# Neighbourhood attention in a hybrid layer: the value products of the tile behind move behind the scores of the next tile in TensorE's order

## The chip, the cores and the metric

The kernel runs on one core of a Trainium2 chip. The metric is the device time of one execution in microseconds (us). TensorE (PE, with its weight loads as PEld), VectorE (DVE), ScalarE (ACT), GpSimd (POOL) and SyncE (SP, which issues the DMAs) each work through a queue of their own.

## The reference, cut to what matters

The layer projects 1024 tokens and 16 meta tokens, runs latent attention (MLA) over 8 heads and neighbourhood attention (NA) over 16 heads of 64, gates both, projects and adds. The change is in the neighbourhood attention: each token of a 16 x 64 grid sees a window of 8 rows x 16 columns and the meta tokens.

```python
def row_block(args):
    r, q_row = args
    ...
    s_win = (jnp.einsum('bqhd,brqchd->bhqrc', q_row, k_win).astype(jnp.float32) * scale
             + bias.astype(jnp.float32)[None])
    s_meta = jnp.einsum('bqhd,bmhd->bhqm', q_row, k_meta).astype(jnp.float32) * scale + meta_b
    s = jnp.concatenate([s_win.reshape(B, NA_HEADS, GRID_W, n_win), s_meta], axis=-1)
    p = jax.nn.softmax(s, axis=-1).astype(v.dtype)
    ...
    return (jnp.einsum('bhqrc,brqchd->bqhd', p_win, v_win)
            + jnp.einsum('bhqm,bmhd->bqhd', p_meta, v_meta))
```

## The kernel before, in words

The program has a gate and setup stage (up to about 217 us), the neighbourhood stage (217 to 700 us), which the change touches, the latent attention and the output projection. Where operands are split, a rounded part (`h`, written by ScalarE, L481, L612, L158) and its rest (`l`, the difference, written by VectorE through the helper at L114) are multiplied apart, so that one product takes two or three matmuls.

The neighbourhood stage goes through 8 head pairs of 8 tiles of 128 queries: 64 tiles. Its loop (L718) takes one *step* per tile and overlaps several tiles in it. In step g:

- tile g+6 is projected to q, k and v (`part`, 24 matmuls into `ps_acc`, cut into the pieces 0 to 1, 1 to 4 and 4 to 8 of the 8 input chunks: 3, 9 and 12 matmuls). Its q and k are normalised (`na_acc`, `na_acc2`);
- tile g+3 has its q and k transposed (`na_tr`, `ps_tr<-raw`). ScalarE and VectorE split them: keys into `kM` (L481, rests at L114), queries into `qz` and `qs`;
- tile g+1 gets its scores (`na_qk`, `ps_s<-kM`, four matmuls, two for each head). They need the keys of the tile behind it, which `na_tr` transposed at the end of the step before. VectorE adds the bias and takes the minimum (L587), ScalarE takes the exponential (L592);
- tile g has its probabilities transposed, head by head (`na_ptr`, `ps_tr<-s_sb`); ScalarE casts them into `PT` (L612), VectorE writes their rest (L114). There are two `PT` buffers for each head, taken by turns (`PTS[j][t % 2]`);
- tile g-1 gets its value products (`na_pv`, L616, `ps_o<-PT`, six matmuls of 128 x 256). After every second tile ScalarE copies half of each bank (`u_na`, L638) and VectorE adds three times (L639, L640).

At the end of steps 3 and 7 of a pair the softmax sums of four tiles are spread and transposed too (`na_sum2`, `ps_tr<-rx`, copied by ScalarE as `nrp`, L662), and in step 1 the meta tokens are projected. The weights of the next pair are loaded and split (`w_split`, L151 to L160) over four steps. A step is numbered here by the tile that it projects, 0 to 7 in each pair.

What sets the order: TensorE's order is the order in which the program is written (`manual_schedule` for that engine alone). The queues of the other engines are ordered when the program is built, by a scheduler that starts from the order of the program and from times that it assumes, so a move on TensorE moves instructions on the others. Banks of PSUM: `ps_s` and `ps_tr` share four (tag `st`), `ps_o` has two and `ps_acc` two. A bank is taken again when its readers are done.

Of the kernel before, what the change touches and what calls it, by code (L numbers as in the profile page):

```python
# [21 lines left out]
NT = 8  # L22
# [27 lines left out]
def hybrid_layer(ctx, tc, x, x_t, meta, meta_t, norm_w, w_na, w_g, w_lat, lat_w, w_uq, w_ukv, vec128, qpe_w, kpe_w,  # L50
# [65 lines left out]
    def mm(o, l, r, start, stop):  # L116
        T.matmul(o, lhsT=l, rhs=r, start=start, stop=stop, skip_group_check=True)  # L117
# [323 lines left out]
    PTS = [[np1.tile([P, 3, 2, P], F32R, name=f"PT{j}{k}") for k in range(2)] for j in range(2)]  # L441
# [130 lines left out]
    def na_qk(p, t):  # L572
        d = st[p]
        w = WE if edge(t) else WI
        k0 = KS * max(t - 1, 0) + NM
        bias = d["b0"] if t == 0 else d["b7"] if t == NT - 1 else d["bi"]
        if t % 4 == 0:
            d["sum", t // 4] = small.tile([P, 4, 2], F32, name="nsum", bufs=2)
        qz, qs = d["q"][t]
        for j in range(2):  # L580
            s_ps = bank("s")[:, :w]
            mm(s_ps, qz[:, j], d["kM"][:, j, k0:k0 + w], True, False)
            mm(s_ps, qs[:, j], d["kM"][:, j, k0:k0 + w], False, True)
            sb = np2.tile([P, WI], F32, name="s_sb", bufs=3)[:, :w]

            mn = small.tile([P, 1], F32, name="nmn")
            V.tensor_tensor_reduce(out=sb, in0=s_ps, in1=bias[:, j, :], scale=1.0, scalar=BIG,  # L587
                                   op0=ALU.add, op1=ALU.min, accum_out=mn)
            d["p", t, j] = sb, mn
        for j in range(2):  # L590
            sb, mn = d["p", t, j]
            S.activation(sb, sb, AF.Exp, scale=-1.0, bias=mn, accum_out=d["sum", t // 4][:, t % 4, j:j + 1])  # L592

    def na_ptr(p, t, j):

        d = st[p]
        sb = d["p", t, j][0]
        ps = bank("tr")[:, :384].rearrange("p (c n) -> p c n", c=3)
        pt = d["PT", j] = PTS[j][t % 2]
        if not edge(t):  # L600

            for n, c in enumerate((0, 272, 144)):
                tr(ps[:, n, :], sb[:, c:c + P])
            parts = ((P, 0, 3),)
        else:

            for n, c in enumerate((144, 0) if t == 0 else (0, 144)):
                tr(ps[:, n, :], sb[:, c:c + P])
            tr(ps[:NM, 2, :], sb[:, 128:144])
            parts = ((P, 0, 2), (NM, 2, 3))  # L610
        for n, c0, c1 in parts:
            S.copy(pt[:n, c0:c1, 0, :], ps[:n, c0:c1])  # L612
        for n, c0, c1 in parts:
            lo_of(pt[:n, c0:c1, 1, :], ps[:n, c0:c1], pt[:n, c0:c1, 0, :])

    def na_pv(p, t):  # L616
        d = st[p]
        i = t % 2
        if i == 0:
            d["o"] = [bank("o").rearrange("p (t n) -> p t n", t=2) for _ in range(2)]  # L620
        if edge(t):
            vs = ((d["V"][1 if t == 0 else t - 1], P), (d["V"][t], P), (d["Vm"], P))
        else:
            vs = ((d["V"][t - 1], P), (d["Vp", t], P), (d["V"][t], P))
        for j in range(2):
            for n, (v, k) in enumerate(vs):
                sm = v.rearrange("p (j a) d -> p j (a d)", j=2)
                mm(d["o"][j][:, i, :], sm[:k, j, :], d["PT", j][:k, n].rearrange("p a n -> p (a n)"), n == 0, n == 2)
        if i == 1:

            if t % 4 == 1:
                d["y", t // 4] = np2.tile([P, 4, P], F32, name="y_na")
            y = d["y", t // 4][:, t % 4 - 1:t % 4 + 1]
            u = np2.tile([P, 2, 2, P], F32, name="u_na", bufs=1)
            for j in range(2):
                a, b = slice(64 * j, 64 * j + 64), slice(64 - 64 * j, 128 - 64 * j)
                o = d["o"][j].rearrange("p t (a n) -> p t a n", a=2)
                S.copy(u[a], o[b])  # L638
                V.tensor_tensor(u[a], u[a], o[a], op=ALU.add)  # L639
            V.tensor_tensor(y, u[:, :, 0, :], u[:, :, 1, :], op=ALU.add)  # L640
# [77 lines left out]
    for g in range(-LEAD, NSTEP + 4):  # L718
        a, b, pr = g, g - 1, g + LEAD
        on = lambda s: 0 <= s < NSTEP  # L720
        part = lambda c0, c1: None
        p, t = divmod(pr, NT)
# [15 lines left out]
            na_meta2(p)  # L738
        if on(b - 1) and (b - 1) % 4 == 3:
            na_sum((b - 1) // NT, (b - 1) % NT // 4)  # L740
        if on(b):
            na_pv(*divmod(b, NT))
        if on(pr - 2) and pr % 2:
            na_acc2(*divmod(pr - 2, NT))
        if on(a):
# [1 line left out]
        part(1, 4)  # L747
        if on(a + 1):
            na_qk(*divmod(a + 1, NT))
        if on(a):  # L750
            na_ptr(*divmod(a, NT), 1)
        part(4, 8)
# [2 lines left out]
        if on(pr):  # L755
# [8 lines left out]
            if 1 < t < 6:  # L764
                k = t - 2
# [146 lines left out]
    for i in range(LEAD, NT + 1):  # L912
        t = order[i]
# [96 lines left out]
    with ExitStack() as mx_:  # L1010
# [116 lines left out]
        for s in range(NS + 3):  # L1127
            cur = s < NS
            h, t = divmod(s, NT)
# [8 lines left out]
            if NS - 10 <= s < NS - 3:  # L1138

                i = s - (NS - 10)  # L1140
                k = KO[i]
# [63 lines left out]
    with ExitStack() as ox:  # L1205
# [21 lines left out]
        for i, k in enumerate(KO[7:]):  # L1227
            if i == 0:
                a, b = KH[:, :D], KL[:, :D]
            elif i == 1:  # L1230
                a, b = (mk.tile([P, L], F32R, name=f"wok{j}", tag=f"mkT{j}")[:, :D] for j in range(2))
            elif i == 2:
                v = mk.tile([P, NT + 1, 2, P], F32R, name="wov", tag="mV").rearrange("p k a n -> p (k a n)")
                a, b = v[:, :D], v[:, D:2 * D]
            else:
                a = o1.tile([P, D], F32R, name=f"woh{k}")
                b = o1.tile([P, D], F32R, name=f"wol{k}")
# [124 lines left out]
```

## Time and profile before

| | |
|---|---|
| median of 3 runs | 1369.73 us (1367.43 to 1370.75) |
| the profiled execution's own time | 1367.42 us |
| its span, first to last instruction | 1365.6 us |
| mean granted clock of TensorE | 0.989 |
| busy share of the span | PE 96%, DVE 70%, ACT 59%, POOL 29% |
| neighbourhood stage, 225 to 650 us | a head pair takes some 61 us; TensorE busy 402.4 of 425 us |

Times in the trace count from the start of the span. Matmuls are pipelined: one of 384 columns is shown with 340 ns, the next starts 176 ns after it, so what a piece takes is read from start to start. The idle time in brackets behind an instruction counts from the shown end of the one before. The granted clock is a share of 2.4 GHz; 0.5 is the lower level, 1.2 GHz.

### The profile page before, as it was taken

What the parts mean: (1) busy time and instruction counts of PE and PEld (TensorE: products, weight loads), DVE (VectorE), ACT (ScalarE), POOL (GpSimd) and SP (SyncE); (2) the same over time, 40 slices, a digit from 0 to 9 for tenths busy, and PEclk for the clock granted to TensorE, in tenths of its full rate; (3) what the DMA queues carried; (4) which work ended last, traced back from release to release, by engine and by line L of the source; (5) the groups of instructions that cost most, each with busy time, mean ns of one, the idle gap of its engine ahead of it and who ended that gap; (6) DMA issues with size and microseconds to landing.
All of it is one profiled execution on the core that took longest, in us unless ns stands there. A gap on an engine that the chain in (4) does not pass through costs nothing.

```text
span 1365.6 us, 24617 instructions
## 1 busy us (share of the span) xinstructions
PE 1312.9 (96%) x8116; PEld 1212.4 (89%) x8116; DVE 962.3 (70%) x3100; ACT 808.7 (59%) x2263; POOL 402.2 (29%) x851
## 2 busy tenths in 40 slices
PE   9999999999999999999899889999999999999999
PEld 7888889889898988989789889999999999988887
DVE  4933246888888888888778988988997988641110
ACT  6622136677776778677756667777777777630110
POOL 4322112122121222112345536625734752000000
PEclk9999999999999999999999899999999999999999
DMA  9352641131212212111111110100100022254231
GB/s 342 124 172 81 210 138 40 54 88 44 74 41 74 67 55 79 59 56 32 51 49 38 43 36 17 40 28 21 36 28 24 31 82 76 78 171 130 73 105 47
DMA packets 82254, 103.59 MB, mean 76 GB/s; under 512 B 10311, under 2 KB 60871, under 8 KB 82007
## 3 DMA queue, kind: packets, MB, share of 16 engines
q1 hardware_dynamic: 82127, 102.02, 23.8%
q8 instruction: 64, 1.05, 0.3%
q14 instruction: 63, 0.52, 0.1%
HBM read 70.80 MB, written 24.90 MB: 70 GB/s over the span
## 4 chain that ended last, share of the span: by engine, by line
PE 71%; DVE 17%; ACT 5%; issue 3%; DMA 2%; POOL 1%; SPq 0%; ACTq 0%; POOLq 0%; DVEq 0%
PE ps_acc L117 20%; PE mps_acc L117 10%; PE ps_s L117 9%; PE mps_s L117 8%; PE mps_st L117 7%; PE mps_o L117 5%; PE ps_o L117 5%; PE mps_tr L120 4%; PE ps_tr L120 3%; DVE u_na L639 2%; DVE m_sb L1034 2%; DMA wnf<-in_w_na_dram 1%; DVE PT L114 1%; DVE qs L557 1%; ACT qz L554 1%
## 5 line engine op out<-in xcount | busy, mean ns | idle before, releaser
L93 POOL TENSOR_TENSOR rs_y<-rs_v,mhalf 128x1 f32<-128x1 f32 (+5 forms) x170 | 148.5, 877 | 119.0 <-DVE rs_v L89 92.4
L117 PE MATMUL ps_acc<-wnh,hT 128*128 128x384 f32 (+1 forms) x432 | 161.7, 374 | 1.5 <-DVE natl L681 1.5
L117 PE MATMUL ps_acc<-wnl,hT 128*128 128x384 f32 (+1 forms) x432 | 146.0, 338 | 0.0
L117 PE MATMUL ps_acc<-wnh,hTl 128*128 128x384 f32 (+1 forms) x432 | 145.6, 337 | 0.0
L558 POOL CAST qs<-qz 64x128 fp32r<-64x128 f32 x128 | 42.1, 329 | 321.3 <-ACT qz L554 310.2
L117 PE MATMUL mps_s<-mkT,mq 128*128 128x346 f32 (+1 forms) x576 | 132.6, 339 | 1.4 <-DVE mPT L114 1.0
L592 ACT ACTIVATE s_sb<-s_sb,nmn 128x400 f32<-128x400 f32 (+1 forms) x128 | 76.9, 601 | 59.6 <-DVE nmn L587 51.5
L1060 ACT CAST mPT<-mps_tr 128x512 fp32r<-128x512 f32 x128 | 74.4, 583 | 53.7 <-PE mps_tr L120 52.7
L117 PE MATMUL mps_o<-mPT,mV 128*128 128x256 f32 x768 | 106.2, 287 | 0.0
L1034 DVE TENSOR_SCALAR_CACHE_REDUCE m_sb<-mps_s 128x346 f32<-128x346 f32 (+1 forms) x192 | 97.3, 512 | 9.7 <-PE mps_s L117 7.5
L114 DVE TENSOR_TENSOR mPT<-mps_tr,mPT 128x512 fp32r<-128x512 f32 x128 | 87.6, 685 | 13.6 <-ACT mPT L1060 12.5
L117 PEld LDWEIGHTS mps_s<-mkT,mq 128*128 128x128 f32 x576 | 93.7, 193 | 3.2 <-DVE mPT L114 1.7
L117 PEld LDWEIGHTS mps_o<-mPT,mV 128*128 128x128 f32 x768 | 94.8, 189 | 0.2
L1043 ACT ACTIVATE m_sb<-m_sb,mnm 128x1040 f32<-128x1040 f32 x64 | 74.6, 1166 | 20.9 <-DVE mnm L1042 14.8
L117 PEld LDWEIGHTS ps_acc<-wnh,hT 128*128 128x128 f32 x432 | 83.3, 193 | 2.6 <-DVE natl L681 1.7
L117 PEld LDWEIGHTS ps_acc<-wnl,hT 128*128 128x128 f32 x432 | 83.3, 193 | 0.0
L117 PEld LDWEIGHTS ps_acc<-wnh,hTl 128*128 128x128 f32 x432 | 82.5, 191 | 0.0
L612 ACT CAST PT<-ps_tr 128x384 fp32r<-128x384 f32 (+2 forms) x160 | 62.1, 411 | 31.1 <-PE ps_tr L120 30.1
L120 PE MATMUL mps_tr<-ident,m_sb 128*128 128x128 f32 x512 | 76.9, 273 | 2.6 <-DVE mq L114 1.0
L114 DVE TENSOR_TENSOR PT<-ps_tr,PT 128x384 fp32r<-128x384 f32 (+2 forms) x160 | 72.1, 466 | 7.0 <-ACT PT L612 6.1
L117 PE MATMUL ps_o<-PT,Vt 128*128 128x256 f32 x256 | 60.1, 298 | 15.9 <-DVE PT L114 15.9
L114 POOL TENSOR_TENSOR wnl<-wnf,wnh 128x384 fp32r<-128x384 f32 (+2 forms) x62 | 53.0, 874 | 61.2 <-ACT wnh L160 55.0
(477 smaller groups left out, 3931.1 us busy)
## 6 DMA issues: line engine op xcount, KB each, us to landing
wnf<-in_w_na_dram SPq DMA_DIRECT2D x32, 384.0 KB, 3.3
g_d<-g SPq DMA_DIRECT2D x32, 256.0 KB, 2.6
wnf<-in_w_out_dram SPq DMA_DIRECT2D x32, 256.0 KB, 2.7
wnf<-in_w_g_dram SPq DMA_DIRECT2D x19, 384.0 KB, 5.5
Vp<-Vt SPq DMA_DIRECT2D x48, 112.0 KB, 2.2
yfo<-y_d SPq DMA_DIRECT2D x24, 192.0 KB, 2.8
gt<-g_d SPq DMA_DIRECT2D x16, 256.0 KB, 3.1
y_d<-y_na SPq DMA_DIRECT2D x16, 256.0 KB, 2.0
```

Of the source, the lines that this page charges most:

```text
L93: G.tensor_tensor(y, v, mhalf[:np_, :n], op=ALU.pow)
L114: eng.tensor_tensor(dst, src, f(hi), op=ALU.subtract)
L117: T.matmul(o, lhsT=l, rhs=r, start=start, stop=stop, skip_group_check=True)
L120: T.transpose(out=o, in_=i, identity=ident[: i.shape[0], : i.shape[0]])
L554: lambda: [S.activation(qz[i, j], ps[i, :P], AF.Copy, scale=qkwn[i]) for j, i in enumerate((slice(0, 64), slice(64, P)))])
L558: G.tensor_copy(qs[h_, j], qz[l_, j])
L592: S.activation(sb, sb, AF.Exp, scale=-1.0, bias=mn, accum_out=d["sum", t // 4][:, t % 4, j:j + 1])
L612: S.copy(pt[:n, c0:c1, 0, :], ps[:n, c0:c1])
L639: V.tensor_tensor(u[a], u[a], o[a], op=ALU.add)
L1034: V.tensor_scalar(st["sb", h, t][:, ks], s_ps, -SCALE, BIG, op0=ALU.mult, op1=ALU.min, accum_out=st["mx", h, t][:, b:b + 1])
L1043: S.activation(sb, sb, AF.Exp, scale=-1.0, bias=nm, accum_out=st["ms", h, t // 2][:, t % 2:t % 2 + 1])
L1060: S.copy(dh, ps)
```

## The change

In a step the value products of the tile behind (`na_pv`) come after the scores of the next tile (`na_qk`) and not before the transposes of head 0. Since the step's own `na_ptr` for head 0 now comes before them in the program, the dictionary that holds `PT` is keyed by the buffer too.

```diff
@@ na_ptr
-        pt = d["PT", j] = PTS[j][t % 2]
+        pt = d["PT", j, t % 2] = PTS[j][t % 2]
@@ na_pv
-                mm(d["o"][j][:, i, :], sm[:k, j, :], d["PT", j][:k, n].rearrange("p a n -> p (a n)"), n == 0, n == 2)
+                mm(d["o"][j][:, i, :], sm[:k, j, :], d["PT", j, i][:k, n].rearrange("p a n -> p (a n)"), n == 0, n == 2)
@@ the loop over steps
-        if on(b):
-            na_pv(*divmod(b, NT))
         if on(pr - 2) and pr % 2:
             na_acc2(*divmod(pr - 2, NT))
         if on(a):
...
         part(1, 4)
         if on(a + 1):
             na_qk(*divmod(a + 1, NT))
+        if on(b):
+            na_pv(*divmod(b, NT))
         if on(a):
             na_ptr(*divmod(a, NT), 1)
```

TensorE's order in step 1 of a head pair, before. The first row is the transpose that ends step 0; numbers are buffers (they differ between the two programs), `PT00` and `PT10` are the `PT` buffers of the two heads:

```order
L120 MATMUL ps_tr_3924<-ident_62,raw_3540 128x128 x2
...
L117 MATMUL ps_acc_3948<-wnh_3328,hTl0_94 128x384
L117 MATMUL ps_o_3952<-PT00_1661,Vt_3197 128x256
...
L117 MATMUL ps_o_3953<-PT10_1663,Vt_3313 128x256
L120 MATMUL ps_tr_3965<-ident_62,s_sb_3895 128x128 x3
L117 MATMUL ps_acc_3948<-wnh_3328,hT0_92 128x384
...
L117 MATMUL ps_s_3981<-kM_3027,qz2_1653 128x400
...
L117 MATMUL ps_s_3987<-kM_3027,qs_3827 128x400
L120 MATMUL ps_tr_3995<-ident_62,s_sb_3901 128x128 x3
```

And the same step now:

```order
L120 MATMUL ps_tr_3924<-ident_62,raw_3540 128x128 x2
...
L117 MATMUL ps_acc_3948<-wnh_3328,hTl0_94 128x384
L120 MATMUL ps_tr_3957<-ident_62,s_sb_3882 128x128 x3
L117 MATMUL ps_acc_3948<-wnh_3328,hT0_92 128x384
...
L117 MATMUL ps_s_3973<-kM_3027,qz2_1653 128x400
...
L117 MATMUL ps_s_3979<-kM_3027,qs_3827 128x400
L117 MATMUL ps_o_3987<-PT00_1661,Vt_3197 128x256
...
L117 MATMUL ps_o_3988<-PT10_1663,Vt_3313 128x256
L120 MATMUL ps_tr_3995<-ident_62,s_sb_3888 128x128 x3
```

The six value products moved behind nine projections, three transposes and the four scores; all else stands as it did.

VectorE's queue from the key rests of step 7 (first row) to those of step 0 (last row), before. `wnl` and `wnlx` are the weights' rests, `ISA` is the addition of the bias with the minimum (L587), `u_na` and `y_na` belong to the value products:

```order
L114 TENSOR_TENSOR kM_3027<-ps_tr_3824,kM_3027 64x128 x2
...
L114 TENSOR_TENSOR wnl_4381<-wnf_4378,wnh_4380 128x384
...
L639 TENSOR_TENSOR u_na_3871<-u_na_3871,ps_o_3764 64x512
L587 ISA s_sb_3895,nmn_3896<-ps_s_3892,bi_3658 128x400
...
L639 TENSOR_TENSOR u_na_3871<-u_na_3871,ps_o_3765 64x512
...
L587 ISA s_sb_3901,nmn_3902<-ps_s_3898,bi_3658 128x400
...
L114 TENSOR_TENSOR PT00_1661<-ps_tr_3877,PT00_1661 128x3x128
L114 TENSOR_TENSOR wnlx_4483<-wnf_4480,wnhx_4482 128x384
L114 TENSOR_TENSOR PT10_1663<-ps_tr_3906,PT10_1663 128x3x128
L640 TENSOR_TENSOR y_na_3870<-u_na_3871 128x256
...
L114 TENSOR_TENSOR kM_3027<-ps_tr_3924,kM_3027 64x128 x2
```

And now:

```order
L114 TENSOR_TENSOR kM_3027<-ps_tr_3824,kM_3027 64x128 x2
...
L114 TENSOR_TENSOR wnl_4381<-wnf_4378,wnh_4380 128x384 x2
...
L587 ISA s_sb_3882,nmn_3883<-ps_s_3879,bi_3658 128x400
...
L114 TENSOR_TENSOR PT00_1661<-ps_tr_3864,PT00_1661 128x3x128
L587 ISA s_sb_3888,nmn_3889<-ps_s_3885,bi_3658 128x400
...
L114 TENSOR_TENSOR wnlx_4483<-wnf_4480,wnhx_4482 128x384 x2
...
L639 TENSOR_TENSOR u_na_3900<-u_na_3900,ps_o_3798 64x512
L639 TENSOR_TENSOR u_na_3900<-u_na_3900,ps_o_3799 64x512
L114 TENSOR_TENSOR PT10_1663<-ps_tr_3906,PT10_1663 128x3x128
...
L114 TENSOR_TENSOR kM_3027<-ps_tr_3924,kM_3027 64x128 x2
```

The scheduler put the rest of head 0's `PT` and the scores' reductions ahead of `u_na`, one weight rest more into the stretch, and `y_na` behind it (it follows the last row).

ScalarE's queue around the key casts of step 7 (`kM`, then `qz`), before:

```order
L460 CAST Vt_3840<-ps_acc_3754 128x2x64
L158 CAST wnh_4380<-wnf_4378 128x384
L481 CAST kM_3027<-ps_tr_3824 64x128 x2
L554 ACTIVATE qz2_1653<-ps_tr_3824,qkw_na_1649 64x128 x2
L158 CAST wnh_4380<-wnf_4378 128x384
L662 COPY nrp_3854<-ps_tr_3849 128x512
```

And now:

```order
L460 CAST Vt_3840<-ps_acc_3754 128x2x64
L481 CAST kM_3027<-ps_tr_3824 64x128 x2
L554 ACTIVATE qz2_1653<-ps_tr_3824,qkw_na_1649 64x128 x2
L158 CAST wnh_4380<-wnf_4378 128x384 x2
L662 COPY nrp_3854<-ps_tr_3849 128x512
```

The weight cast that stood ahead of the key casts stands behind them, next to its other half.

## Rows read from the trace of the kernel before

**Rows 1.** The page, busy time of each engine over the whole span, its share, and how many instructions.

```profile
PE 1312.9 (96%) x8116; PEld 1212.4 (89%) x8116; DVE 962.3 (70%) x3100; ACT 808.7 (59%) x2263; POOL 402.2 (29%) x851
```

**Rows 2.** Who waited for whom, TensorE's own waits between 195 and 700 us (microseconds in total, times, the longest).

```profile
PE ps_o L117 <- DVE PT L114: 15.9, 13, 2.1
PE ps_s L117 <- DVE kM L114: 5.4, 7, 2.4
PE ps_tr L120 <- DVE PT L114: 3.9, 7, 0.6
```

**Rows 3.** TensorE in order of time in one head pair (start in us, duration, engine, line, operation, tiles, shape, count; in brackets the idle time before and who ended it). `ps_acc` is a projection, `ps_o` the value products, `ps_s` the scores (with `hM`: the meta tokens' projection), `ps_tr` a transpose. The rows at 351.32, 359.10, 371.93, 399.20 and 405.73 are the first of steps 0, 1, 2, 6 and 7.

```profile
347.59 0.34 PE L117 MATMUL ps_s<-kM,qz 128*128 128x400 f32 x1
...
351.32 0.42 PE L117 MATMUL ps_acc<-wnh,hT 128*128 128x384 f32 x1
...
351.93 0.27 PE L117 MATMUL ps_o<-PT,Vt 128*128 128x256 f32 x1
...
352.74 0.49 PE L120 MATMUL ps_tr<-ident,s_sb 128*128 128x128 f32 x3
...
355.22 0.46 PE L117 MATMUL ps_s<-kM,qz 128*128 128x400 f32 x1 [0.42 <-DVE kM L114]
...
356.05 0.45 PE L117 MATMUL ps_s<-kM,qz 128*128 128x400 f32 x1 [0.19 <-ACT nrp L662]
...
359.10 0.42 PE L117 MATMUL ps_acc<-wnh,hT 128*128 128x384 f32 x1
...
361.96 0.39 PE L117 MATMUL ps_o<-PT,Vt 128*128 128x256 f32 x1 [2.09 <-DVE PT L114]
...
362.89 0.58 PE L117 MATMUL ps_o<-PT,Vt 128*128 128x256 f32 x1 [0.31 <-DVE PT L114]
...
369.98 0.36 PE L117 MATMUL ps_s<-wnh,hM 128*48 128x256 f32 x1
...
371.93 0.34 PE L117 MATMUL ps_acc<-wnh,hT 128*128 128x384 f32 x1
...
392.55 0.44 PE L120 MATMUL ps_tr<-ident,raw 128*128 128x128 f32 x2 [0.55 <-DVE PT L114]
...
399.20 0.42 PE L117 MATMUL ps_acc<-wnh,hT 128*128 128x384 f32 x1
...
402.43 0.34 PE L117 MATMUL ps_s<-kM,qz 128*128 128x400 f32 x1
...
405.73 0.42 PE L117 MATMUL ps_acc<-wnh,hT 128*128 128x384 f32 x1
```

**Rows 4.** TensorE by stretch (the stretch, its length, busy time and instructions, granted clock as a share of 2.4 GHz, share of the DMA engines, GB/s), behind waits in four head pairs.

```profile
243.00:247.00 4.00, 3.97 (x26) 1.00 0.46 131
301.00:305.00 4.00, 2.70 (x17) 1.00 0.74 221
362.00:366.00 4.00, 3.69 (x15) 0.57 0.69 187
546.00:550.00 4.00, 3.55 (x14) 0.61 0.57 165
```

**Rows 5.** One stretch by engine (the stretch, its length, then busy time and instructions of PE, PEld, DVE, ACT and POOL, granted clock, DMA share, GB/s).

```profile
354.88:363.28 8.40, 5.47 (x29) 4.54 (x30) 8.13 (x22) 7.21 (x19) 1.67 (x5) 0.96 0.42 120
```

**Rows 6.** VectorE in order of time in the same head pair: the rests of the keys' split, two instructions (one for each head) in a row; the one at 388.36 is of the meta tokens' keys.

```profile
346.75 0.61 DVE L114 TENSOR_TENSOR kM<-ps_tr,kM 64x128 fp32r<-64x128 f32 x2 [0.48 <-ACT qz L554]
...
354.88 0.61 DVE L114 TENSOR_TENSOR kM<-ps_tr,kM 64x128 fp32r<-64x128 f32 x2 [0.65 <-ACT qz L554]
...
388.36 0.59 DVE L114 TENSOR_TENSOR kM<-ps_tr,kM 64x128 fp32r<-64x128 f32 x2
...
401.30 0.61 DVE L114 TENSOR_TENSOR kM<-ps_tr,kM 64x128 fp32r<-64x128 f32 x2 [0.66 <-ACT qz L554]
```

**Rows 7.** ScalarE in order of time at the end of step 7 and in step 0 of the same head pair.

```profile
352.52 0.28 ACT L460 CAST Vt<-ps_acc 128x128 fp32r<-128x128 f32 x1
...
353.13 0.51 ACT L158 CAST wnh<-wnf 128x384 fp32r<-128x384 f32 x1 [0.33 <-DMA wnf<-in_w_na_dram]
...
353.55 0.53 ACT L481 CAST kM<-ps_tr 64x128 fp32r<-64x128 f32 x2
...
355.41 0.59 ACT L662 COPY nrp<-ps_tr 128x512 f32<-128x512 f32 x1
```

**Rows 8.** Groups of VectorE's instructions between 348 and 410 us (count, busy us, mean ns of one, idle us before them).

```profile
L114 DVE TENSOR_TENSOR wnl<-wnf,wnh 128x384 fp32r<-128x384 f32 x6 | 3.2, 552 | 0.3 <-ACT wnh L158 0.3
...
L640 DVE TENSOR_TENSOR y_na<-u_na 128x256 f32<-128x256 f32 x4 | 1.6, 412 | 0.0
```

**Rows 9.** TensorE in order of time, single waits in other head pairs.

```profile
243.03 0.39 PE L117 MATMUL ps_o<-PT,Vt 128*128 128x256 f32 x1 [1.46 <-DVE PT L114]
...
301.99 0.38 PE L117 MATMUL ps_o<-PT,Vt 128*128 128x256 f32 x1 [2.10 <-DVE PT L114]
...
601.44 0.45 PE L117 MATMUL ps_s<-kM,qz 128*128 128x400 f32 x1 [1.12 <-DVE kM L114]
...
660.73 0.45 PE L117 MATMUL ps_s<-kM,qz 128*128 128x400 f32 x1 [2.42 <-DVE kM L114]
...
666.13 0.42 PE L117 MATMUL ps_o<-PT,Vt 128*128 128x256 f32 x1 [1.53 <-DVE PT L114]
```

**Rows 10.** The same view as rows 8 for ScalarE between 225 and 700 us.

```profile
L638 ACT COPY u_na<-ps_o 64x512 f32<-64x512 f32 x64 | 37.2, 581 | 5.0 <-PE ps_o L117 3.6
```

## The prediction

> **What bounds the kernel now.** I read the engines' busy shares first, then TensorE's waits, then one head pair of the neighbourhood stage in order of time, then the clock and the other engines in the stretch where TensorE waits. TensorE is busy 96% of the span [rows 1], so a change pays only where TensorE stands still or runs slowly. Between 195 and 700 us it stands still before its value products for 15.9 us in 13 places, always for the rest part of the transposed probabilities (`PT`) from VectorE; before the scores 5.4 us for the rest part of the keys (`kM`); before the transposes 3.9 us for `PT` [rows 2]. [rows 3] are one head pair. I name a step by the tile it projects, 0 to 7. A step without a wait takes 405.73 - 399.20 = 6.53 us. Step 0 takes 359.10 - 351.32 = 7.78, so 1.25 too long (waits of 0.42 and 0.19, the rest restarts). Step 1 takes 371.93 - 359.10 = 12.83, of which 371.93 - 369.98 = 1.95 are meta products: 4.35 too long. In it stand the waits of 2.09 and 0.31, and a slow clock behind them: over 362 to 366 us the granted clock is 0.57 [rows 4], the half level of 1.2 GHz for most of it, which loses 4 x 0.43 = 1.7 us. The reader is to see that this step holds nearly all. Step 4 has the 0.55 at 392.55. Excess of the pair: 1.25 + 4.35 + 0.55 = 6.15 us.
>
> Why it waits: in steps 7 to 1 VectorE also splits the next head pair's weights. From the key rests at 354.88 to the next ones at 363.28 it is busy 8.13 of 8.40 us [rows 5], and the `PT` that the value products want stands late among that work.
>
> **The change part by part.** The value products (six matmuls, 352.74 - 351.93 = 0.81 us [rows 3]) move behind part 1 to 4 of the projection, the transposes of head 0 and the scores. TensorE's work is the same to the instruction.
>
> *What goes.* The value products now start later by what went ahead: from step start to scores 402.43 - 399.20 = 3.23 us, less 0.81 of their own and the first part's 0.6 that was ahead anyway, plus the scores' 0.73, is 2.5 us. Step 1's waits of 2.09 + 0.31 are below that, so by this alone they end. The 0.55 in step 4 waits for a PSUM bank that `PT` of head 0 still holds; 0.81 more lies between now, so it ends too.
>
> *What comes.* The scores come 0.81 us earlier and need the key rests from the step before. VectorE has the same work between two key rests, so the question is when that work starts and how it is queued.
> Step 7: scores were at 347.59 without a wait; at 346.78 they meet key rests that begin at 346.75 [rows 6] and take 0.61 for both heads, half of it for the first: wait 0.3, with restart 0.4.
> Step 0: before, ScalarE's key casts stood behind a weight cast that waited for its DMA (353.13), and began at 353.55 [rows 7]. In the changed order they come straight behind the `Vt` cast of 352.52, so at about 352.7, 0.85 earlier, and VectorE's key rests, which began 1.33 behind the casts, begin at 354.0 in place of 354.88. The scores (moved to 353.9) wait 0.3. The second head's scores wait for the bank that ScalarE frees with the copy `nrp`. It now stands behind both weight casts (0.42 each from start to start), which follow at 354.0, and takes 0.59: done at 355.4, where TensorE would be at 354.6. That wait grows from 0.19 to 0.8. With restarts 1.3, about as before.
> Step 1: VectorE's list from key rests to key rests loses a `y_na` (0.41) and gains a weight split (0.55 [rows 8]); a small `rs_y` that leaves and a small reciprocal that comes cancel. It is 8.5 us in place of 8.4, so the next key rests begin at 354.0 + 8.5 = 362.5 and the first head's are there at 362.8. TensorE reaches the scores at 351.6 (step 0's start, 0.3 late from step 7) + 6.53 + 1.3 + (3.23 - 0.81) = 361.8. Wait 1.0, with restart 1.1; then the value products follow at once, since their `PT` stands ahead of the key rests in the changed list. That is what is late next: the wait's owner changes and its size falls.
> Step 4: scores meet the meta keys' rests (388.36 [rows 6]), which read the bank that the second head wants: 0.8 in place of 0.55.
> Steps 2, 3, 5 and 6: the tightest is step 6, whose first head's key rests end at 401.30 + 0.3 = 401.6 [rows 6], 0.8 before its scores at 402.43: nothing.
> After: 0.4 + 1.3 + 1.1 + 0.8 = 3.6 us in place of 6.15.
>
> *The clock.* Behind waits of 2.1 it fell in four pairs (0.57 in the first, 0.61 in the last, over 4 us: some 1.6 us each), behind the 2.10 at 301.99 and the 1.46 at 243.03 it stayed at 1.00 [rows 4, 9]. A wait of 1.0 is nearest to the last: I price it at nothing; the other end is 1.6 us a pair.
>
> *The new wait's bounds.* The scores' wait for `kM` in step 1 is bounded below by the 0.42 of step 0 [rows 3], above by the 2.42 at 660.73 [rows 9], where ScalarE too was behind a DMA. The queue above gives 1.0; 0.4 would give 3 us more over five pairs, 2.4 with the slow clock takes the gain of step 1 away (rival 1).
>
> *What rides along.* Every second value step brings two ScalarE copies and three VectorE additions (`u_na`, `y_na`), which move with it; in the list above they are counted, behind the scores' reductions rather than ahead. It issues no DMA. The stores of `y` and loads of the gate follow `y_na` on SP's queue by some us, and nobody waits for them in this stage; `Vp` is wanted later than before. The `Vt` buffer that the value products free is next written after part 4 to 8, whose twelve matmuls lie between: hidden.
>
> *A rule against it.* These gaps repeat every head pair. The Trainium skill (Perfetto Trace Analysis, Optimization Strategy) says that the same gap repeating can mean that there is no SBUF or PSUM room for the next tile; by that a new order gives nothing and buffers are wanted. The trace agrees for the 0.55 (a bank), not for the 2.09, whose releaser is the data itself.
>
> **The sum.** Four pairs with the slow clock: 4 x (6.15 - 3.6) = 10.2. The pair at 302, without it: 0.9. The first pair has the 1.46 and a wait like the 0.55: I take half, 1.0. The pair at 601: its scores already wait 1.12 for `kM`, which grows by 0.8, and what goes before its value products and transposes is of that size: 0. The last tiles: the scores' 2.42 keeps its end, behind it the 1.53 at 666.13 goes, and a wait for key rests like step 1's comes, but the slow clock there may stay: 1.0 as an estimate between 0 and 1.9 (the 1.53 with a restart). Together 13.1. The profiled execution took 1367.4 us: 1354.3. It lay 2.3 us under the median of the runs (1369.7), so 1356.6, **1357 us**, for a median.
>
> **The rivals.**
> 1. *VectorE keeps the wait.* It works through 8.4 us without a gap whatever TensorE's order is; if its key rests of step 1 end as late as before (363.28 + 0.61 = 363.9 where TensorE wants them at 361.8), the scores wait 2.1 and the clock falls as it did. For it: the busy share of that stretch [rows 5]. Against it: the key casts are no longer behind the DMA. Then a pair gains 0 to 0.3, all in all 2 us: 1368. The Trainium skill (Perfetto Trace Analysis, Identifying the Most-Contended Engine) says to relieve the most-contended engine first; by that a new order on TensorE alone would give nothing. The trace agrees as far as the busy share of these steps goes.
> 2. *All waits end.* If ScalarE and VectorE run ahead since their inputs come 0.81 earlier, nothing replaces the 15.9 + 3.9 and the clock's 4 x 1.6: 26 us, 1344. Against it: the key rests.
> 3. *Slower: the `u_na` copies get ahead of the key casts.* In the changed order ScalarE's two copies out of PSUM (0.58 each [rows 10]) lie between scores and the step's key casts. If they wait for late value products and hold the key casts back by more than the 0.8 or so that the quiet steps have, each of the four steps a pair with copies loses about 0.81 + 1.16 - 0.8 = 1.2: 7 pairs x 4.7 = 33, less rival 2's 26: 7 us longer, 1377. For it: the copies' place. Against it: in the quiet steps ScalarE has gaps.
>
> **How the numbers follow.** Forecast 0.60, rival 1 0.20, rival 2 0.10, rival 3 0.10. A measurement of this kernel can tell about 0.3%, 4 us. The forecast and rival 2 are faster: 0.70; rival 1 the same: 0.20; rival 3 slower: 0.10. The forecast's own range is 1351 to 1363 (the new wait at 0.4 takes 3 off, all of the last tiles' waits 2 or so; the clock at its other end adds 6.5). To 8 in 10 the range takes in rival 1 and stops short of 2 and 3: 1347 to 1368.
>
> **What would show it.** Right: TensorE's waits before the value products near 0; before the scores for `kM` 12 to 16 us in 15 or more places, the longest of a regular pair near 1.0 us in step 1; granted clock 1.00 where it was 0.97; no wait of 0.55 before the transposes of step 4; `kM` casts on ScalarE ahead of the weight cast. Wrong: scores' waits of 2 us with a clock of 0.57 behind them (rival 1), or waits in steps 2, 3, 5 and 6 (rival 3).

## The result and the profile after

The changed kernel takes **1344.85 us** (median of 4 runs, 1344.31 to 1345.33) against 1368.88 of the kernel before beside it: ratio 0.983, interval 0.9817 to 0.9843. The profiled execution took 1344.79, 22.6 less than that of before. It is faster, as forecast, but by 24 us and not by 13, and it lies 2 us below the range. The time is that of rival 2, which had a chance of 0.10. The page and TensorE's own waits of after (microseconds, times, the longest), the counterparts of [rows 1, 2]:

```profile
span 1343.0 us, 24641 instructions
PE 1301.1 (97%) x8116; PEld 1202.7 (90%) x8116; DVE 956.9 (71%) x3100; ACT 806.5 (60%) x2263; POOL 398.2 (30%) x851
```

```profile
PE ps_s L117 <- DVE kM L114: 10.4, 10, 2.8
```

The 15.9 us before the value products are gone without a remainder, and so are the 3.9 before the transposes for `PT`. Before the scores 10.4 us for the keys stand in place of 5.4, in 10 places (the prediction's signs had 12 to 16 us in 15 or more). TensorE in order of time in the pair that answers to [rows 3]; the rows of `raw` are the transposes of queries and keys that end a step in both orders, here those that end steps 6, 7, 0 and 1 and the next step 6:

```profile
339.11 0.38 PE L120 MATMUL ps_tr<-ident,raw 128*128 128x128 f32 x2
...
341.75 0.36 PE L117 MATMUL ps_s<-kM,qz 128*128 128x400 f32 x1
...
345.68 0.38 PE L120 MATMUL ps_tr<-ident,raw 128*128 128x128 f32 x2
...
348.76 0.34 PE L117 MATMUL ps_s<-kM,qz 128*128 128x400 f32 x1
...
349.63 0.43 PE L117 MATMUL ps_s<-kM,qz 128*128 128x400 f32 x1 [0.35 <-DVE qs L557]
...
353.21 0.38 PE L120 MATMUL ps_tr<-ident,raw 128*128 128x128 f32 x2
...
356.89 0.45 PE L117 MATMUL ps_s<-kM,qz 128*128 128x400 f32 x1 [0.88 <-DVE kM L114]
...
360.88 0.38 PE L120 MATMUL ps_tr<-ident,raw 128*128 128x128 f32 x2
...
396.19 0.38 PE L120 MATMUL ps_tr<-ident,raw 128*128 128x128 f32 x2
```

Step 7 has no wait, step 0 one of 0.35 before the second head's scores, step 1 one of 0.88 for the keys, and nothing stands before the value products. The 0.35 ends with `qs`, VectorE's rests of the queries just transposed. These scores use queries that were transposed a step earlier, so by this reading they wait for a bank that `qs` reads, not for data. Behind the 0.88 the clock stays (stretch, length, then busy time and instructions of PE, PEld, DVE, ACT, POOL, granted clock, DMA share, GB/s), where [rows 4] had 0.57:

```profile
357.00:361.00 4.00, 4.00 (x27) 3.82 (x28) 3.92 (x13) 1.96 (x6) 0.00 (x0) 1.00 0.32 119
```

From one `raw` to the next I get the length of every step, in both kernels and all experiments (us, the pair at 340 to 410):

| kernel | step 7 | 0 | 1 | 2 | 3 | 4 | 5 | 6 | pair |
|---|---|---|---|---|---|---|---|---|---|
| before | 6.54 | 8.21 | 10.88 | 8.39 | 6.54 | 7.78 | 6.51 | 6.54 | 61.39 |
| changed | 6.57 | 7.53 | 7.67 | 8.39 | 6.52 | 7.33 | 6.50 | 6.57 | 57.08 |
| e1 value products late, scores as before | 6.54 | 7.68 | 7.82 | 8.39 | 6.53 | 7.08 | 6.86 | 6.52 | 57.42 |
| e2 move in step 1 alone | 6.55 | 8.16 | 8.64 | 8.38 | 6.53 | 7.78 | 6.47 | 6.53 | 59.04 |
| e3 move in all but step 1 | 6.57 | 7.55 | 8.70 | 8.40 | 6.52 | 7.31 | 6.51 | 6.57 | 58.13 |
| e4 changed, one chunk later | 6.79 | 7.58 | 7.73 | 8.37 | 6.52 | 7.79 | 6.28 | 6.54 | 57.60 |
| e4b changed, one chunk earlier | 6.70 | 7.15 | 8.45 | 8.42 | 6.88 | 7.72 | 7.37 | 7.09 | 59.78 |
| e5 changed, splits on GpSimd | 6.59 | 8.97 | 10.39 | 8.41 | 6.52 | 7.32 | 6.53 | 6.57 | 61.30 |
| e6 before, splits on GpSimd | 6.54 | 10.02 | 10.85 | 8.41 | 6.55 | 7.79 | 6.51 | 6.56 | 63.23 |
| e7 e1, both one chunk later | 6.50 | 6.99 | 7.96 | 8.59 | 6.50 | 7.00 | 6.59 | 6.51 | 56.64 |
| e8 changed, value products further back | 6.78 | 6.96 | 8.44 | 8.41 | 6.83 | 7.45 | 7.41 | 6.90 | 59.18 |
| e9 e1, scores alone a chunk later | 7.13 | 7.48 | 8.01 | 8.51 | 7.16 | 7.02 | 6.94 | 6.54 | 58.79 |

Over the stage, the same rows at the start of the first pair with the slow clock, behind the four such pairs, and the last of these rows, some steps before the stage ends, of before and (the first row is shown above, at 339.11) of after:

```profile
344.21 0.38 PE L120 MATMUL ps_tr<-ident,raw 128*128 128x128 f32 x2
...
589.83 0.38 PE L120 MATMUL ps_tr<-ident,raw 128*128 128x128 f32 x2
...
678.80 0.38 PE L120 MATMUL ps_tr<-ident,raw 128*128 128x128 f32 x2
```

```profile
567.79 0.38 PE L120 MATMUL ps_tr<-ident,raw 128*128 128x128 f32 x2
...
654.45 0.38 PE L120 MATMUL ps_tr<-ident,raw 128*128 128x128 f32 x2
```

Up to the first row 5.1 us are won (344.21 - 339.11), in the four pairs 16.9 (245.62 against 228.68), from there to the last row 2.3, together 24.35. Behind it 1.75 are lost again: the span ends 686.8 after the last row before, 688.55 now.

### The profile page after: what moved, and what is told of

Its sections match the earlier page's. It is cut to its first block, busy times and chain, and to the rows that moved or that the text cites. A ratio compares the mean times of both kernels' runs of the same rounds, so it can differ in the third digit from the quotient of the medians.

```text
span 1343.0 us, 24641 instructions
## 1 busy us (share of the span) xinstructions
PE 1301.1 (97%) x8116; PEld 1202.7 (90%) x8116; DVE 956.9 (71%) x3100; ACT 806.5 (60%) x2263; POOL 398.2 (30%) x851
## 4 chain that ended last, share of the span: by engine, by line
PE 61%; DVE 20%; ACT 11%; issue 4%; DMA 2%; POOL 1%; SPq 0%; ACTq 0%; DVEq 0%; POOLq 0%
PE ps_acc L117 14%; PE mps_acc L117 10%; PE mps_s L117 8%; PE ps_s L117 8%; PE mps_st L117 7%; PE mps_o L117 5%; PE mps_tr L120 4%; PE ps_o L117 3%; ACT s_sb L592 2%; DVE qs L557 2%; ACT qz L554 2%; PE ps_tr L120 2%; DVE s_sb L587 2%; DVE PT L114 2%; DVE m_sb L1034 2%
## 5 line engine op out<-in xcount | busy, mean ns | idle before, releaser
L558 POOL CAST qs<-qz 64x128 fp32r<-64x128 f32 x128 | 38.3, 299 | 339.5 <-ACT qz L554 327.1
L120 PEld LDWEIGHTS mps_tr<-ident,m_sb 128*128 128x128 f32 x512 | 60.9, 140 | 5.6 <-ACT wnh L160 1.3
```

Source lines behind the costliest of these rows:

```text
L120: T.transpose(out=o, in_=i, identity=ident[: i.shape[0], : i.shape[0]])
L558: G.tensor_copy(qs[h_, j], qz[l_, j])
```

## The experiments

**Theory A**, formed on the two traces: the scores do not meet key rests that stay where they were. The key casts stand on ScalarE behind the exponentials, these behind VectorE's reductions of the scores, so scores that come earlier bring the next step's keys earlier too; the loop moves as a whole. **Theory B**: only the value products' slack counts. **The prediction's rule**: rests stay, so a wait grows by what the scores gain.

**e1.** The value products move, the scores stay (they are behind part 1 to 4, ahead of the scores):

```diff
         part(1, 4)
+        if on(b):
+            na_pv(*divmod(b, NT))
         if on(a + 1):
             na_qk(*divmod(a + 1, NT))
-        if on(b):
-            na_pv(*divmod(b, NT))
```

> Theory A (the loop moves as a whole): scores that come earlier bring the exponentials, the key casts queued behind them on ScalarE, and with these the key rests of the next step earlier too; so moving the scores ahead of the value products costs no wait for keys. Theory B: the value products' slack alone did it, and the scores' place did nothing. Here the value products move behind part 1 to 4 but stay ahead of the scores, so they get 1.7 us of slack and the scores stay where they were. A: step 0 as before (8.1 us, with the waits of 0.3 to 0.45 and 0.2), step 1 about 8.0 (a rest of 0.4 to 0.7 of the wait for PT, then some 0.6 for the keys), step 4 7.3 to 7.8, clock 1.00; head pair 58.1 to 58.7 us, total 1352 to 1356. B: step 0 and 4 as in the changed kernel (7.55 and 7.33), head pair 57.3 to 57.8, total 1345 to 1349.

Measured 1340.59, ratio 0.9812 (0.9794 to 0.983); pair 57.42. The pair is B's, the total is below what either had. TensorE in order of time:

```profile
358.24 0.39 PE L117 MATMUL ps_o<-PT,Vt 128*128 128x256 f32 x1 [0.57 <-DVE PT L114]
```

Of the wait of 2.09 there is 0.57 left, as A said, but step 0 is 0.5 shorter than before though the scores stand where they stood: its wait for `kM` is gone, since ScalarE's weight cast no longer waits for its DMA there. So 4.0 of the 4.3 us that a pair gains come with the value products' move alone, and the scores' earlier place brings the other 0.3. By the ratios this kernel is 0.2% faster than the changed one, which the intervals do not tell apart. In the two traces it is ahead only behind the last row of `raw`, which lies at 655.62, 1.2 later (on what follows there, see e10b).

**e2 and e3.** The move in step 1 alone, and in all but step 1 (against the changed kernel):

```diff
+        if on(b) and pr % NT != 1:      # e3: == 1, at the old place
+            na_pv(*divmod(b, NT))
...
-        if on(b):
+        if on(b) and pr % NT == 1:      # e3: != 1, behind the scores
             na_pv(*divmod(b, NT))
```

> The value products follow the scores in step 1 of each head pair alone; in the other seven steps they stay ahead. If the steps' gains are separate terms, as the prediction summed them, step 1 takes 7.67 us as in the changed kernel, steps 0 and 4 stay at 8.13 and 7.78, head pair 58.1, total about 1352. Theory A: step 0's key rests stay late, VectorE's list of 8.4 us behind them starts late, and the scores of step 1 wait about 1.5 us in place of 0.88; step 1 about 8.3, head pair 58.7, total about 1356, or 1.6 more a pair if the clock falls behind a wait of 1.5 (1366).

> The reverse: the value products stay ahead of the scores in step 1 alone. Separate terms: step 1 keeps its 10.95 us with waits of 2.1 and 0.3 and a clock near 0.57 behind them; steps 0 and 4 at 7.55 and 7.33; head pair 60.3, total about 1362. Theory A: in steps 7 and 0 the scores and what hangs on them come earlier, VectorE's list behind the key rests of step 0 starts about 1 us earlier, so the wait for PT in step 1 falls from 2.1 to about 1.1 and the clock stays at 1.00: step 1 about 8.5 to 9.2, head pair 58 to 58.7, total 1350 to 1355.

Measured 1355.29 (0.9916, 0.9898 to 0.9933) and 1350.59 (0.9882, 0.9864 to 0.9899). Both times are A's. TensorE in step 1 of e2, then of e3 with its clock:

```profile
358.92 0.52 PE L120 MATMUL ps_tr<-ident,s_sb 128*128 128x128 f32 x3 [1.04 <-DVE nmn L587]
...
361.62 0.45 PE L117 MATMUL ps_s<-kM,qz 128*128 128x400 f32 x1 [0.59 <-DVE kM L114]
```

```profile
357.12 0.39 PE L117 MATMUL ps_o<-PT,Vt 128*128 128x256 f32 x1 [0.97 <-DVE u_na L639]
...
358.44 0.39 PE L117 MATMUL ps_o<-PT,Vt 128*128 128x256 f32 x1 [0.69 <-DVE PT L114]
```

```profile
358.00:362.00 4.00, 3.56 (x23) 3.53 (x24) 3.86 (x13) 1.10 (x2) 0.00 (x0) 1.00 0.65 237
```

In e2 step 1 loses 1.04 before the transposes (to the reduction of the scores) and 0.59 before the scores, not one wait of 1.5, since step 0 hands its delay on. In e3 the value products of step 1 stand at the old place, and yet the 2.09 has become 0.97 for the sums' additions (`u_na`) and 0.69 for `PT`, and the clock stays; in one of five pairs with these waits it fell (0.72 over 534 to 540 us). A pair gains 2.35 in e2 and 3.26 in e3, 5.6 together, where the whole move gains 4.3: the steps are no separate terms. The prediction carried step 0's keys into step 1, but took step 0's own keys from no step before it.

**e4 and e4b.** The changed kernel with scores and value products one chunk later, and one earlier:

```diff
-        part(1, 4)
+        part(1, 5)      # e4b: part(1, 3)
...
-        part(4, 8)
+        part(5, 8)      # e4b: part(3, 8)
```

> The changed kernel with scores and value products one chunk of the projection (three matmuls, 0.5 us) later. If the key rests stay where they are (the prediction's rule), step 1's wait of 0.88 for the keys falls to about 0.4 and step 0's 0.35 ends: 0.8 us a head pair, total about 1339 to 1341. Theory A: the key rests come 0.5 later with the scores, the wait in step 1 stays at 0.8 to 0.9 and that of step 0 at 0.3; total 1344 to 1347; the gap between key rests and scores in the quiet steps, 0.1 us in the changed kernel, grows to about 0.6.

> The changed kernel with scores and value products one chunk of the projection (0.5 us) earlier. Theory A with a floor: the keys of a step begin with its last transposes, and in the quiet steps the key rests already stand 2.24 us behind these with the scores 0.1 behind the first head's rest; 0.5 earlier the scores wait about 0.4 in each of the 60 steps, total 1362 to 1370. Theory A without a floor (all moves along): 1343 to 1347. The prediction's rule (rests fixed where they were): waits of 0.4 in the quiet steps and 1.3 in step 1, 1366 to 1373.

Measured 1345.67 (0.9843, 0.9826 to 0.986) and 1359.43 (0.9937, 0.9916 to 0.9958). In e4, step 0's key casts (ScalarE) and rests (VectorE), and the scores of steps 0 and 1:

```profile
348.63 0.54 ACT L481 CAST kM<-ps_tr 64x128 fp32r<-64x128 f32 x2
```

```profile
349.97 0.61 DVE L114 TENSOR_TENSOR kM<-ps_tr,kM 64x128 fp32r<-64x128 f32 x2 [0.52 <-ACT qz L554]
```

```profile
351.46 0.42 PE L117 MATMUL ps_s<-kM,qz 128*128 128x400 f32 x1 [0.40 <-DVE qs L557]
...
358.75 0.45 PE L117 MATMUL ps_s<-kM,qz 128*128 128x400 f32 x1 [0.89 <-DVE kM L114]
```

Against the transposes at 346.93 the casts come at 1.70 and the rests at 3.04; in the changed kernel (345.68) at 1.12 and 2.47. With scores 0.52 later the keys come 0.58 later, and the waits are 0.40 and 0.89 in place of 0.35 and 0.88. That is A, to a tenth, and against the prediction's rule. It holds in steps 7 to 1; in the quiet step behind the transposes at 391.20 the rests hardly move (2.32 us behind these, 2.24 in the changed kernel). e4b shows the floor:

```profile
394.13 0.40 PE L117 MATMUL ps_s<-kM,qz 128*128 128x272 f32 x1 [0.62 <-DVE kM L114]
...
401.13 0.45 PE L117 MATMUL ps_s<-kM,qz 128*128 128x400 f32 x1 [0.28 <-DVE kM L114]
```

With scores 0.5 earlier the key rests of these two quiet steps begin 2.60 and 2.24 us behind the transposes (391.19 and 398.56), no earlier than in the changed kernel (2.27 and 2.24), and the scores wait 0.62 and 0.28. It costs less than I had set (15 us and not 18 to 25), since not every step waits.

**e5, e6, e10.** Half of the next pair's weight splits on GpSimd in place of VectorE, in the changed kernel, in the kernel before and in e1:

```diff
-        d["w"].append(w_split(w_na[p, :, 2 * k:2 * k + 2, :], 384, (V, V), parts=True, own=wx if k == 3 else None))
+        d["w"].append(w_split(w_na[p, :, 2 * k:2 * k + 2, :], 384, (V, G), parts=True, own=wx if k == 3 else None))
```

> The changed kernel with the second half of each weight split of the next head pair on GpSimd in place of VectorE (four of eight splits a pair, 0.55 us each on VectorE). If what is left, 0.88 us before the scores of step 1 and 0.35 in step 0, is VectorE's backlog of splits: one to two splits less lie between the key rests of steps 0 and 1, the 0.88 falls to 0 to 0.3, step 1 about 6.9, head pair 56.2 to 56.5, total about 1338 to 1341. If it is TensorE's or ScalarE's chain that sets the keys: unchanged, 1344 to 1347. Rival: GpSimd's longer splits hold its copies of the queries back and the scores wait for them: slower, 1348 or more.

> The same on the kernel before, the value products ahead of the scores. If VectorE's backlog makes the wait of 2.1 before the value products of step 1: it falls by two to three splits to 0.5 to 1.0, the clock stays 1.00 in that step, step 1 about 8.3 to 8.8 in place of 10.95, head pair 58.5 to 59.5, total 1352 to 1358. If the wait is set by the place of the value products alone: 2.0 or more and a clock near 0.57 as before, total 1366 to 1370.

> The version with the value products behind part 1 to 4 and ahead of the scores, with the same splits on GpSimd. If the backlog makes its 0.57 before the value products of step 1: it ends, step 1 about 7.0 to 7.3, head pair 56.5 to 57, total about 1334 to 1338, the fastest so far. Else 1340.

Measured 1359.1 (0.994, 0.9924 to 0.9956), 1369.62 (1.0017, 1.0006 to 1.0028) and 1352.74 (0.9892, 0.9875 to 0.9908; no trace of it is read). None brings what a shorter list on VectorE was to bring: they lie 18, 12 and 15 us above that. The time of e5 is in its rival's range (1348 or more), but its scores wait for keys and not for queries. That of e6 is in the range for "the place of the value products alone", though the longest wait before these is 1.5 and not 2.0. e10 lies 13 us above even its other branch. Step 0 of e5 on ScalarE, its scores of steps 0 and 1 on TensorE, and the clock behind them:

```profile
353.88 0.52 ACT L158 CAST wnh<-wnf 128x384 fp32r<-128x384 f32 x1 [0.39 <-DMA wnf<-in_w_na_dram]
```

```profile
355.97 0.45 PE L117 MATMUL ps_s<-kM,qz 128*128 128x400 f32 x1 [1.30 <-DVE kM L114]
...
365.24 0.45 PE L117 MATMUL ps_s<-kM,qz 128*128 128x400 f32 x1 [2.04 <-DVE kM L114]
```

```profile
365.00:369.00 4.00, 3.76 (x16) 3.67 (x17) 3.00 (x11) 1.31 (x4) 0.00 (x0) 0.61 0.18 67
```

This is, in the changed order of TensorE, what the prediction feared: a weight cast that waits 0.39 for its DMA ahead of the key casts, which follow at 354.30, keys late in step 0 (1.30), late again in step 1 (2.04), and the slow clock. GpSimd takes 1.1 us in the mean for a split that VectorE does in 0.55; that the weight's buffer is thus free later for the next load would explain the waiting cast, but is not shown. VectorE gained nothing either (e5, VectorE, then GpSimd):

```profile
358.03 0.97 DVE L100 TENSOR_TENSOR rs_t<-rs_y 128x8 f32<-128x8 f32 x1
```

```profile
357.64 1.33 POOL L114 TENSOR_TENSOR wnlx<-wnf,wnhx 128x384 fp32r<-128x384 f32 x1
```

The 8-column `rs_t`, 0.16 us in the changed kernel, takes 0.97 and ends at 359.00, with GpSimd's split (358.97). In e6 the same happens (a split on VectorE takes 1.36, `rs_t` 0.97), the transposes at the end of step 0 wait 1.56 for the reduction of the scores, and the pair is 1.8 longer than before (others 0.5 to 1.0). So whether VectorE's backlog alone makes the 2.09 is left open by these three; what e5 shows is how much one waiting cast ahead of the key casts, with VectorE's list stretched behind it, brings back.

**e7, e8, e9.** e1 with value products and scores one chunk later; the changed kernel with the value products behind the second head's transposes; e1 with the scores alone a chunk later:

```diff
-        part(1, 4)
+        part(1, 5)      # e7, on e1; then part(5, 8)
...
         if on(a):
             na_ptr(*divmod(a, NT), 1)
+        if on(b):       # e8, on the changed kernel
+            na_pv(*divmod(b, NT))
...
         if on(b):
             na_pv(*divmod(b, NT))
+        part(4, 5)      # e9, on e1; then part(5, 8)
         if on(a + 1):
             na_qk(*divmod(a + 1, NT))
```

> Value products ahead of the scores, both one chunk later than in the version of the first study (behind part 1 to 5 of the projection). Theory A: the scores' place costs nothing as long as they stand behind the floor, and the value products get 0.5 us more slack, so the 0.57 before them in step 1 falls to 0 to 0.2: step 1 about 7.3, head pair 56.8 to 57.1, total 1336 to 1339 (the stage behind this one taken as in that version). If the wait for PT is carried by the scores' place (later scores, later exponentials, later PT), it stays 0.5 to 0.6: head pair 57.4, total 1340.

> The changed kernel with the value products one place further back, behind the transposes of the second head. Theory A: they wait for nothing already, so more slack gives nothing; the scores and their wait of 0.88 in step 1 stay; the transposes of the second head come 0.8 earlier, which could meet the bank they write. Head pair 56.9 to 57.4, total 1341 to 1347. If VectorE's queue gets the copies of the sums out of the keys' way, step 1's wait falls to 0.4 and the total to 1340.

> As the version with the value products behind part 1 to 4 and ahead of the scores, with one chunk of the projection between the two, so the scores alone come 0.5 us later. Theory A: nothing changes in the first place, head pair 57.3 to 57.6, total 1339 to 1343; the key casts and rests of the next step come up to 0.5 later with the scores. If the rests stay fixed, the 0.57 before the value products would not change either, but the 0.2 before step 0's scores would end: 57.2.

Measured 1339.9 (0.9797, 0.9781 to 0.9814), 1353.13 (0.9891, 0.9872 to 0.991) and 1348.31 (0.986, 0.9842 to 0.9878). e7 has the shortest pair, 56.64, and in it no wait before value products or scores, as A had it. The pair is 0.2 under A's range though step 1 took 7.96 and not 7.3, and the total 1 us over it, at the other branch's 1340. e8 and e9 miss. TensorE's waits in e7 and in e9:

```profile
PE ps_tr L120 <- ACT s_sb L592: 5.5, 8, 0.8
```

```profile
PE ps_tr L120 <- ACT s_sb L592: 14.8, 28, 0.9
```

In e9 the first head's transposes of the next step wait for the exponentials in 28 places. That is not the price of late scores: in step 6 these begin 3.87 us behind the transposes in e7 (338.43 - 334.56) and 3.86 in e9 (339.17 - 335.31), and only in e9 does the wait follow. What differs is VectorE's queue. Its first reduction of these scores, in e7 and in e9:

```profile
340.00 0.56 DVE L587 CUSTOM_DVE_ANT_0 s_sb<-ps_s,bi 128x400 f32<-128x400 f32 x1
```

```profile
341.67 0.57 DVE L587 CUSTOM_DVE_ANT_0 s_sb<-ps_s,bi 128x400 f32<-128x400 f32 x1
```

It begins 5.44 us behind the transposes in e7, with one addition of `u_na` ahead of it, and 6.36 in e9, with both. So A has a floor; that it has a ceiling is not shown.

In e8 the keys of step 1 come later (a wait of 1.21), and the transposes of the second head, now straight behind the scores, start late in most steps. One of them on TensorE, and what ends just before it on VectorE:

```profile
377.53 0.52 PE L120 MATMUL ps_tr<-ident,s_sb 128*128 128x128 f32 x3
```

```profile
376.67 0.71 DVE L557 SCALAR_TENSOR_TENSOR qs<-ps_tr,qkw_na,qz 64x128 fp32r<-64x128 f32 x2
```

The last score is at 377.11, so this is 0.42 behind it, and 0.15 behind the end of `qs`. Of 57 such places between 225 and 650 us 44 start more than 0.3 behind the last score, and 36 of these are 0.15 behind the end of `qs`. The profile names the scores for them, but in the kernel before, where these transposes stand behind the scores too, 54 of 56 follow in 0.12 to 0.20. So what they meet is, by this reading, the bank that `qs` reads, as the expectation feared.

**e10b.** e7, but with `part(1, 4)` in the last eight steps:

```diff
-        part(1, 5)
+        cs = 5 if a < NSTEP - 8 * 1 else 4
+        part(1, cs)
...
-        part(5, 8)
+        part(cs, 8)
```

> Value products ahead of the scores, behind part 1 to 5 of the projection as in the version with both one chunk later, but behind part 1 to 4 in the last eight steps, where that version waited 1.5 for the normalised projections. If what that version lost behind the neighbourhood stage (a first transpose of the next stage that waits 3.9 us for the queries' rests, 1.4 in the version with part 1 to 4) hangs on the order of the last steps, total 1335 to 1338, the fastest. If not: 1338 to 1341.

Measured 1338.96 (0.9794, 0.9781 to 0.9808), the lowest time of all, some 0.4% under the changed kernel by the ratios, but not told from e7 and e1 by the intervals; it still loses the 3.9 us behind the stage, so the order of the last steps does not decide those. What does shows only in part. The first transpose of the next stage, before and after:

```profile
759.60 0.66 PE L120 MATMUL mps_tr<-ident,natl 128*128 128x128 f32 x2 [1.41 <-DVE mq L114]
```

```profile
737.41 0.66 PE L120 MATMUL mps_tr<-ident,natl 128*128 128x128 f32 x2 [3.58 <-DVE mq L114]
```

The 2.17 between them is more than the 1.75 lost behind the stage. VectorE's order is the same there; TensorE goes on behind the second of three rests (`mq`) in one, behind the third in the other. e1 and e2 wait 1.41 there, e3, e4, e7 and e10b 3.9 to 4.0, e5, e8 and e9 not at all. Why is open, and was not tried.

## Why the prediction was right in its sign and wrong in its size

- **What goes: right.** The waits before the value products and the 0.55 in step 4 end.
- **The clock: right.** It stays at 1.00, and its price was: step 1 of the pair at 302, with the same waits and no fall [rows 4, 9], was 9.45 us long, in the others 10.9, so 1.5 where I set 1.6.
- **Step 1: right.** Forecast 4.35 of excess to 1.1, so 3.25 won; measured 10.88 - 7.67 = 3.21, with a wait of 0.88 for 1.0. That the wait came out is in part luck: counted from the transposes that end step 7, its keys and TensorE both came about half a microsecond earlier than forecast. VectorE's list from key rests to key rests takes 8.40 for my 8.5:

```profile
348.15 0.61 DVE L114 TENSOR_TENSOR kM<-ps_tr,kM 64x128 fp32r<-64x128 f32 x2 [0.48 <-ACT qz L554]
...
356.55 0.61 DVE L114 TENSOR_TENSOR kM<-ps_tr,kM 64x128 fp32r<-64x128 f32 x2
```

- **Step 0: wrong, and the step of the prediction that failed is "they come straight behind the `Vt` cast of 352.52, so at about 352.7, 0.85 earlier".** ScalarE after, then the two rows of before that stand ahead of [rows 7]:

```profile
345.51 0.63 ACT L592 ACTIVATE s_sb<-s_sb,nmn 128x400 f32<-128x400 f32 x1
...
346.13 0.37 ACT L530 ACTIVATE sqn<-ps_acc 128x256 f32<-128x256 f32 x1
...
346.65 0.28 ACT L460 CAST Vt<-ps_acc 128x128 fp32r<-128x128 f32 x1
...
346.80 0.54 ACT L481 CAST kM<-ps_tr 64x128 fp32r<-64x128 f32 x2
...
349.17 0.59 ACT L662 COPY nrp<-ps_tr 128x512 f32<-128x512 f32 x1
```

```profile
351.38 0.63 ACT L592 ACTIVATE s_sb<-s_sb,nmn 128x400 f32<-128x400 f32 x1 [0.24 <-DVE nmn L587]
...
352.00 0.36 ACT L530 ACTIVATE sqn<-ps_acc 128x256 f32<-128x256 f32 x1
```

Counted from the transposes (345.68, and 350.75 before), the key casts come at 1.12 in place of 2.80, 1.68 earlier. The waiting weight cast accounts for the time between `Vt` and the casts, 0.15 for 1.03, so 0.88 as forecast. The other 0.80 is that all that stands ahead, from the exponential on, comes earlier (`sqn` at 0.45 in place of 1.25). The exponential stands behind VectorE's second reduction of the scores of step 7 (L587), and this at the end of a list without a gap. VectorE before, then after:

```profile
348.81 1.01 DVE L114 TENSOR_TENSOR wnl<-wnf,wnh 128x384 fp32r<-128x384 f32 x2
...
350.24 0.55 DVE L114 TENSOR_TENSOR wnl<-wnf,wnh 128x384 fp32r<-128x384 f32 x1
350.71 0.56 DVE L587 CUSTOM_DVE_ANT_0 s_sb<-ps_s,bi 128x400 f32<-128x400 f32 x1
```

```profile
341.32 0.61 DVE L114 TENSOR_TENSOR kM<-ps_tr,kM 64x128 fp32r<-64x128 f32 x2 [0.22 <-ACT qz L554]
...
343.38 0.55 DVE L114 TENSOR_TENSOR wnl<-wnf,wnh 128x384 fp32r<-128x384 f32 x1
...
344.34 0.56 DVE L114 TENSOR_TENSOR wnl<-wnf,wnh 128x384 fp32r<-128x384 f32 x1
344.81 0.57 DVE L587 CUSTOM_DVE_ANT_0 s_sb<-ps_s,bi 128x400 f32<-128x400 f32 x1
```

The reduction begins 0.87 ahead of the transposes in place of 0.04. Of these 0.83, 0.36 is that the key rests that open the list come earlier (4.36 ahead for 4.00, the 346.75 of [rows 6]), and 0.47 that two weight rests stand before it and not three. The scores themselves had been there for some 2 us: in the changed kernel VectorE waits for scores nowhere between 225 and 650 us. So the earlier scores did not bring the keys by ending a wait; they did it through the order of the other engines' queues, which is made anew for every order of TensorE. No run held these queues as they were, so what the new order of TensorE would do alone is open. I moved the demand by 0.81 and left the supply. e4 shows that keys follow the scores' place. So no wait for `kM` came in step 0, none in step 7 (0.4 forecast), and step 0 fell by 0.68 where I had it stay.
- **The second head's scores: wrong by an owner taken over.** I took the profile's `nrp` in [rows 3] for what frees their bank in the new order too, and priced 0.8 in step 0 and as much in step 4, for the meta keys. In the kernel before they start 0.05 or 0.06 behind the end of `nrp` in all five such pairs, so that reading stands. After the change they start at 349.63, before `nrp` ends (349.17 + 0.59 = 349.76) and 0.15 behind the end of `qs`, with a wait of 0.35; step 4 has no such wait and is 0.45 shorter. In e5, with the same order on TensorE, it is `nrp` again (0.20). The name beside a wait in one program need not hold in another.
- **The sum.** A pair: forecast 2.55, measured 4.31; step 7 (0.4), step 0 (0.7) and step 4 (0.7) are the difference. Over the four pairs 16.9 for 10.2, up to them 5.1 for 1.9, behind them 2.3 for 1.0, and behind the last transposes of the stage -1.75 for 0: 22.6 for 13.1.
- **The rivals.** Rival 1 is out: VectorE's list is as long as it said, but it starts earlier. Rival 2 gave the time, and was nearer to the reason: ScalarE and VectorE do run ahead, though by their queues' order rather than by inputs that they had waited for. Its time is in part luck, since it had nothing replace the waits, and those for the keys grew by 5.0 us (10.4 for 5.4). I set the key rests against it, which are part of the loop that moves. Rival 3 did not come: in the quiet steps the `u_na` copies do lie between the scores and the key casts, but these begin as close behind the transposes as before (340.01 - 339.11 = 0.90; before, 338.55 - 337.67 = 0.88). The Trainium skill (Perfetto Trace Analysis, Optimization Strategy) has too little buffer room as a possible cause of a bubble that repeats; here an order with the same buffers ended them, the 0.55 on a bank included.

## What to carry to other kernels

Where an operation of a loop is moved, follow the loop round once before a supplier's time is taken over from the old trace: here what the moved scores hand on moved with them, and their wait did not grow by what they were moved. In this kernel that went through the queues of VectorE and ScalarE, which are ordered anew for every order of TensorE, so compare these queues too, from what stands ahead of the supplier. Such a place has a floor (what feeds the loop from outside, here the transposes of the keys). The slack belongs to the side branch, here the value products: their move alone gave most of the gain. Places that differ by one piece on TensorE still gave 1339 to 1359 us, since the other queues changed with them. Work on an idle engine is not free if it slows the busy one.

## What the runs showed of the hardware

- Small VectorE operations stretch beside GpSimd: 0.16 to 0.97 us for 8 columns in e5, and the weight splits of 128 x 384 left on VectorE (`wnl`) from 569 ns in the mean in the changed kernel to 826. The Trainium skill (SBUF — State Buffer, SBUF: two separate sides) says that a VectorE operation with two SBUF inputs and a GpSimd operation that reads SBUF lock a shared pair of ports, the first to start for its whole instruction. `rs_t` has two SBUF inputs, and the trace agrees: it ends with GpSimd's split.
- The clock does not follow the single wait: 0.57 to 0.61 behind some 2.1 in four pairs and 1.00 behind 2.10 in one [rows 4, 9]; 1.00 in four pairs of e3 behind 0.97 and 0.69, and 0.72 over 534 to 540 us behind the same in a fifth; 0.50 over 363 to 367 us in e6, behind 1.56 and 1.51.
- A transpose right behind the scores starts 0.12 to 0.20 us after the last of them in 54 of 56 places in the kernel before; where it starts later in e8 it is, in 36 of 44 places, 0.15 behind the end of VectorE's `qs`.
